# Splitting w_out beside the first convolution and loading it back in two parts

## The chip, the core and the metric

The kernel runs on one core of one Trainium2 chip. The metric is device time in microseconds (us): the median of three runs. Besides these runs there is one profiled execution, from which every line of a profile in this document comes.

## What is computed

One layer of an encoder block with two groups of heads, for a prompt of 256 tokens and a sample of 2048, each with 16 meta tokens ahead of it. Width is 1024. Cut to what matters here:

```python
h = rmsnorm(z, norm_w)
q, k, v, g_att, c_val, c_glu, g_conv = split(h @ w_in)
att = windowed_gqa(rmsnorm(q), rmsnorm(k), v, sink) * silu(g_att)      # 8 heads, 2 kv heads, window 128
u   = c_val * sigmoid(c_glu)
cnv = silu(layernorm(depthwise_conv31(u))) * silu(g_conv)
out = z + concatenate([att, cnv], -1) @ w_out                          # w_out: 1024 x 1024
```

All inputs and results are float32. The kernel computes a float32 product in three passes of TensorE: each operand is split into a rounded part (hi) and the rest (lo), and hi·hi, hi·lo and lo·hi are summed (`PASSES`, L125). A split costs one cast on ScalarE (hi) and one subtraction on VectorE (lo).

## The kernel before, in words

**Stages.** There are 18 blocks of 128 tokens, in six groups of three blocks. The first half of the work takes groups 0 to 2, the second half groups 3 to 5. In each half the columns of the input projection are taken in 11 units of 256 columns: four GLU pairs (`U_C`), two units of convolution gates (`U_GC`), two of attention gates (`U_GA`), one of k and v, two of q (`ORDER`). A unit is done for each group of its half (in the first half the first two units alternate by group). A projection is 24 matmuls into one PSUM buffer (L767, or L783 where tokens are the rows); these buffers rotate over two tags of two buffers. A GLU unit's result is multiplied on VectorE (L822), a gate's goes through SiLU on ScalarE (L875, tile `go`, three buffers) and to DRAM. The 31 taps of the convolution are VectorE instructions over 1167 tokens (L841, L850); they run beside the projections, about as many for each projection as its time allows (`tick`, with a credit in ns).

**Weights.** The split of w_in's units is made in the first half and, from the third unit on, kept in DRAM scratch (`wd`, stored in L746, loaded back in the second half in L724, four loads of 512 KB a unit).

**The last unit and the attention.** The last unit of the second half is q's second one. When it starts, the pools of the right side are closed, the attention's tiles are allocated there (`attention_open`), and the attention's first steps are laid between the unit's nine blocks (`spread`). The attention is a pipeline of slots, eight for each block: in step s, block s has its scores (L316, then `bias_max` on VectorE in L371, `expo` on ScalarE in L383, `norm` on GpSimd in L397 and L406), block s-1 has its transposes (L429), their split (L440, L441) and the product with v (L464), and block s-2 has its output projection (L538). `EARLY` is 13: so many slots are laid between the q blocks. The rest follow in `attention_rest`, where the left pools are closed and the tiles for gates, convolution results, x and y are allocated (`bp`). It first loads the first block's attention gate (`load_ga(0)`, L299) and convolution gate and result (`load_mix(0)`, L303 and L305). `mix_conv` (L515) multiplies those two on GpSimd and splits the product (L520, L521).

**w_out.** The output projection needs w_out as hi and lo in SBUF, 16 pieces of 128 x 1024. They lie in six of the tiles that held groups 3 to 5's input (`xh`, `xl` of the pool `xp`; three pieces in a tile), so they can arrive only when a group's last projection is done. `load_wo(n)` is called for row block `OUT_ORDER[n]` behind block 11 (n = 0 to 2), 14 (3 to 5) and 17 (6 and 7), by `WO_AT`. It loads two halves of 256 KB into a tile with two buffers (`woraw`, L290), and two ticks later each is cast (L294) and subtracted (L295) into place.

**Order.** Nearly all DMAs are issued by SyncE (SP), in one order, and all but a few go through one queue over the 16 DMA engines. Tile's planner decides the order of each engine by a simulated timeline with program order as the priority; an instruction in `keep_in_program_order` stays in program order on its engine. From `attention_open` on, GpSimd keeps program order (`MAN1`), and from `attention_rest` on TensorE does too (`MAN2`). An engine that waits holds up everything behind it in its order.

The tags that the change uses are `xt` (four buffers; raw transposed input for a group, loaded in `Prep.load`) and `xn` (two buffers; rows of z in `stats`, used for the sums of squares). Groups 0 to 2 are prepared at the start, groups 3 to 5 at the end of the first half, and `stats` runs in the first units and again in the attention gate units.

Of the kernel before, what the change touches and what calls it, by code (L numbers as in the profile page):

```python
# [10 lines left out]
F32 = mybir.dt.float32  # L11
F32R = mybir.dt.float32r
BF16 = mybir.dt.bfloat16
AF = mybir.ActivationFunctionType
ALU = mybir.AluOpType
AX = mybir.AxisListType

P = 128
D = 1024
# [13 lines left out]
UW = 256  # L33
# [4 lines left out]
XTB = 4  # L38
# [17 lines left out]
PIN_W = 2  # L56
I2 = 2
QP = 2
WO_AT = (3, 3, 3, 4, 4, 4, 5, 5)

GROUPS = [(0, 400)] + [(400 + 384 * i, 384) for i in range(5)]
CHUNKS = [[0, 1, 2], [3, 4, 5]]
# [13 lines left out]
def hymba_kernel(  # L76
# [24 lines left out]
    vmd = dram.tile([NM, 2 * P], F32, name="vmd")  # L101
    wd = dram.tile([11, 4, P, 4 * UW], F32, name="wd")
    cd = dram.tile([NB, P, 512], F32, name="cd")

    ident = const.tile([P, P], F32, name="ident")
    make_identity(nc, ident)
# [29 lines left out]
    def later(k, f):  # L136
        due.setdefault(clock[0] + k, []).append(f)
# [139 lines left out]
    def load_wo(n):  # L277

        e = OUT_ORDER[n]
        for hl in range(2):  # L280
            idx = 2 * n + hl
            if idx % 3 == 0:
                slot = idx // 3
                wo_slot[slot] = xp.tile([P, ND, 400], F32R, tag=("xh", "xl")[slot % 2], name=f"wo{slot}")
            flat = wo_slot[idx // 3].rearrange("p a n -> p (a n)")
            wo[e, hl] = flat[:, D * (idx % 3) : D * (idx % 3) + D]
        for nh in range(2):
            cols = slice(512 * nh, 512 * nh + 512)
            raw = pool["a"].tile([P, 512], F32, tag="woraw", name=f"woraw{n}_{nh}", bufs=2)
            nc.sync.dma_start(raw, w_out[e][:, cols])  # L290
            later(2, lambda hi=wo[e, 0][:, cols], lo=wo[e, 1][:, cols], raw=raw: split_wo(hi, lo, raw))

    def split_wo(hi, lo, raw):
        nc.scalar.copy(hi, raw)  # L294
        nc.vector.tensor_tensor(lo, raw, hi, op=ALU.subtract)  # L295

    def load_ga(b):
        gat[b] = pool["b"].tile([P, 4, P], F32, tag="ga", name=f"ga{b}", bufs=1)
# [2 lines left out]
    def load_mix(b):  # L301
        gct[b] = pool["b"].tile([P, 4, P], F32, tag="gc", name=f"gc{b}")
        nc.sync.dma_start(gct[b], gd[4:8, :, P * b : P * b + P].rearrange("j p n -> p j n"))  # L303
        cnt[b] = pool["b"].tile([P, 4, P], F32, tag="cn", name=f"cn{b}")
        nc.sync.dma_start(cnt[b].rearrange("p j n -> p (j n)"), cd[b])  # L305
# [280 lines left out]
    def spread(b):  # L586

        spread_n[0] += 1
        if spread_n[0] == QP:
            q_prep(0)  # L590
        upto = EARLY * max(0, spread_n[0] - QP) // (9 - QP)
        while len(slots) > len_all - upto:
            slot_step(*slots.pop(0))
        if b % 3 == 2:
            for n in range(8):
                if WO_AT[n] == b // 3:
                    load_wo(n)

# [2 lines left out]
    def attention_rest():  # L601
        while ln_q:
            tick(0)
        for _ in range(2):
            tick(0)
        cst["man"].close()
        att_pools.enter_context(tc.manual_schedule(engines=MAN2))
        left_pools.close()
        pool["b"] = att_pools.enter_context(tc.tile_pool(name="bp", bufs=2, side="left", reuse_waits="tile"))
        load_ga(0)  # L610
        load_mix(0)
        while slots:
            slot_step(*slots.pop(0))
        while work_left():
            tick(3000)
        att_pools.close()

    if True:
# [20 lines left out]
        class Prep:  # L639
# [50 lines left out]
            def split(self, d2):  # L690
                n, xt = self.n, self.xt[d2]
                xh, xl = xg[self.g]
                for dd in range(2):
                    d = 2 * d2 + dd
                    if self.pool:
                        nc.scalar.mul(xh[:, d, :n], xt[:, dd, :n], nw[:, d : d + 1])
                    else:
                        nc.scalar.copy(xh[:, d, :n], xt[:, dd, :n])  # L698
                for dd in range(2):
                    d = 2 * d2 + dd  # L700
                    if self.pool:
                        nc.vector.scalar_tensor_tensor(
                            xl[:, d, :n], xt[:, dd, :n], nw[:, d : d + 1], xh[:, d, :n], op0=ALU.mult, op1=ALU.subtract
                        )
                    else:
                        eng = nc.gpsimd if dd else nc.vector
                        eng.tensor_tensor(xl[:, d, :n], xt[:, dd, :n], xh[:, d, :n], op=ALU.subtract)  # L707
                owe(1000)
# [303 lines left out]
        def at_item_start(i, c, u, g):  # L1012
            if i == 0:
                r[4]()
                r[5]()
                for q in range(4):
                    preps[1].load(q)
                    w01[1][1](q, nc.gpsimd if q % 2 else nc.vector)
                r[6]()
            if i == 1:  # L1020
                later(1, preps[1].first)
                later(1, preps[1].alloc)
                later(1, lambda: preps[1].scale(0))
                for q in range(4):
                    if q < 3:
                        later(1, lambda q=q: preps[1].scale(q + 1))
                    later(1, lambda q=q: preps[1].split(q))
                for k in range(7, 10):
                    later(1, lambda k=k: later(1, stats(k)))
                for q in range(4):  # L1030
                    later(2, lambda q=q: preps[2].load(q))
            if i == I2:
                later(1, preps[2].first)
                later(1, preps[2].alloc)
                later(1, lambda: preps[2].scale(0))
                for q in range(4):
                    if q < 3:
                        later(1, lambda q=q: preps[2].scale(q + 1))
                    later(1, lambda q=q: preps[2].split(q))
# [8 lines left out]
        for i, (c, u, g) in enumerate(items):  # L1048
            if (c, u) == keys[-1] and g == CHUNKS[c][0]:
                while conv_q[0] or conv_q[1]:  # L1050
                    tick(3000)
                for _ in range(3):
                    tick(0)
                right_pools.close()
                attention_open()
            if u in U_C and g == CHUNKS[c][0]:
                u_tiles(c, u)
            ws = wsplit[c, u]
            at_item_start(i, c, u, g)
            for t, p, what in prep_at.get(i, []):  # L1060
                if what == "load":
                    for q in range(4):
                        later(1, lambda p=p, q=q: p.load(q))
                else:
                    later(1, p.first)
                    for q in range(4):
                        later(1 + q // 2, lambda p=p, q=q: p.scale(q))
            if u in U_C:
                c_group(c, u, ws, g)
            elif u in U_Q:  # L1070
                q_group(ws, u - U_Q[0], g, spread if (c, u) == keys[-1] else lambda b: None)
            elif u == U_KV:
                kv_group(ws, g)
            elif u in U_GC:
                g_group(ws, 4 + 2 * (u - U_GC[0]), g)
            else:
                g_group(ws, 2 * (u - U_GA[0]), g)
            for k in loads.get(i, []):
                load, split = weights(k)
                load(nc.sync)  # L1080
                room = max(1, when[first_at[keys[k]]] - when[i + 1])
                for q in range(4):
                    at = max(1, min(room, W0 + q * min(WST, max(1, (room - 2) // 4))))
                    later(at, lambda split=split, q=q: split(q, nc.vector))
            if c == 0 and u in U_GA:
                for k3 in range(3):
                    k = 10 + 3 * (3 * (u - U_GA[0]) + g) + k3
                    if k <= NB:
                        later(1 + k3, lambda k=k: later(1, stats(k)))
            if (c, u) == (0, ORDER[-1]):  # L1090
                p = preps[g + 3]
                p.alloc()
                for q in range(4):
                    later(1 + q // 2, lambda p=p, q=q: p.split(q))
            if u in U_C and g == CHUNKS[c][2]:
                conv(c, u, 0)
            if i == last_at[c, u] and u == U_GC[-1]:
                def ready(c=c):
                    if left[c, 0]:
                        return False  # L1100
                    seen.setdefault(c, clock[0])
                    return clock[0] >= seen[c] + LN_WAIT[c]

                for b in range(0, 8) if c == 0 else range(8, NB):
                    ln_block(c, b, ready)
# [60 lines left out]
```

## Time and profile before

| what | value |
|---|---|
| median of three runs | 976.84 us (975.87 to 977.05) |
| profiled execution, its own time | 974.79 us |
| its span, first to last instruction | 973.0 us |
| busy TensorE / VectorE / ScalarE / GpSimd | 949.2 / 755.9 / 424.6 / 341.2 us |
| mean granted TensorE clock | 0.995 |
| packets' bytes on the DMA queues | 155.75 MB |

How to read the lines: PE is TensorE's matmuls, PEld its weight loads (beside PE), DVE VectorE, ACT ScalarE, POOL GpSimd, SP SyncE; a q behind a name is the engine's sequencer, which issues DMAs. L538 is line 538 of the kernel. A line of the timeline has start, duration, engine, line, operation, output<-input by the program's names, shapes and count; in brackets stands the engine's idle time just before, and what ended it. In the view of waits the columns are total us, times and longest us. In the view by stretches each engine has its busy time and its count of instructions, then come the granted clock (1 is full speed), the mean share of the 16 DMA engines that was busy, and the rate.

### The profile page before, as it was taken

The numbers are of one execution on the slowest core, as the hardware profiler recorded it, in microseconds if no ns is written. First come the engines' busy times: TensorE is split into PE (matmuls) and PEld (weight loads), VectorE is DVE, ScalarE is ACT, GpSimd is POOL, SyncE is SP. The second block draws the span as 40 slices with busy tenths as digits, with TensorE's granted clock in tenths as the row PEclk, the third lists the DMA queues.
The fourth block names the chain that finished last, engine by engine and source line by source line (L and its number), as shares of the span: only waits on it lengthen the run. The fifth ranks groups of instructions, "written<-read, shape, count | busy, mean of one in ns | idle before, by whom it ended". The sixth has DMA issues, their size and how long they took to land.

```text
span 973.0 us, 16234 instructions
## 1 busy us (share of the span) xinstructions
PE 949.2 (98%) x5740; PEld 890.0 (91%) x5740; DVE 755.9 (78%) x1261; ACT 424.6 (44%) x1156; POOL 341.2 (35%) x541
## 2 busy tenths in 40 slices
PE   5999999999999999999999998899999999999998
PEld 5999999999999999999999998678888888888886
DVE  4759999998987699999993555877776777767772
ACT  6621111343468710111113454766665666666651
POOL 5500000364468300000002464745445544544451
PEclk9999999999999999999999998999999999999999
DMA  9643345785735222233335657954554445544321
GB/s 332 221 181 118 130 170 179 264 286 182 225 124 180 92 73 76 86 128 136 127 135 173 212 141 219 294 171 134 159 177 148 125 152 166 178 127 135 109 88 43
DMA packets 113872, 155.75 MB, mean 160 GB/s; under 512 B 10592, under 2 KB 77296, under 8 KB 113792
## 3 DMA queue, kind: packets, MB, share of 16 engines
q1 hardware_dynamic: 113648, 154.11, 48.1%
q0 software_dynamic: 144, 0.62, 0.4%
q8 instruction: 45, 0.74, 0.3%
q14 instruction: 35, 0.29, 0.1%
HBM read 101.00 MB, written 54.31 MB: 160 GB/s over the span
## 4 chain that ended last, share of the span: by engine, by line
PE 91%; DMA 3%; DVE 2%; POOL 1%; issue 1%; SPq 1%; ACT 0%; POOLq 0%; DVEq 0%
PE pj L767 42%; PE y L538 20%; PE pj L783 13%; PE O L464 5%; PE pT L429 4%; PE S L316 4%; DMA woraw<-in_w_out 2%; DMA snk<-in_sink 1%; DMA wraw<-in_w_in 1%; PE O L316 1%; PE lnt L183 1%; PE qT L316 1%; PE lnu L202 1%; PE kt L941 0%; PE pT_m L426 0%
## 5 line engine op out<-in xcount | busy, mean ns | idle before, releaser
L767 PE MATMUL pj<-xh,ws 128*128 128x384 f32 (+1 forms) x1536 | 397.2, 339 | 2.5 <-ACT xh L698 2.5
L850 DVE SCALAR_TENSOR_TENSOR y<-us,cw,y 128x1167 f32<-128x1167 f32 x240 | 329.0, 1428 | 0.6
L767 PEld LDWEIGHTS pj<-xh,ws 128*128 128x128 f32 x1536 | 282.3, 189 | 2.8 <-ACT xh L698 2.8
L767 PE MATMUL pj<-xl,ws 128*128 128x384 f32 (+1 forms) x768 | 262.5, 342 | 0.1
L783 PE MATMUL pj<-ws,xh 128*128 128x256 f32 (+1 forms) x880 | 165.8, 286 | 0.0
L767 PEld LDWEIGHTS pj<-xl,ws 128*128 128x128 f32 x768 | 144.7, 188 | 1.1 <-POOL xl L707 0.7
L783 PEld LDWEIGHTS pj<-ws,xh 128*128 128x128 f32 (+1 forms) x880 | 137.8, 189 | 0.3
L783 PE MATMUL pj<-ws,xl 128*128 128x256 f32 (+1 forms) x440 | 125.4, 285 | 0.0
L383 ACT ACTIVATE sb<-sb,nm 128x304 f32<-128x304 f32 (+4 forms) x144 | 77.1, 535 | 45.3 <-DVE nm L371 43.7
L538 PE MATMUL y<-wo,mch 128*128 128x512 f32 x288 | 95.9, 414 | 0.0
L538 PE MATMUL y<-wo,mah 128*128 128x512 f32 x288 | 93.7, 406 | 0.0
L441 DVE TENSOR_TENSOR pl<-pT,ph 128x512 fp32r<-128x512 f32 x100 | 69.0, 690 | 29.0 <-ACT ph L440 28.5
L875 ACT ACTIVATE go<-pj 128x384 f32<-128x384 f32 x48 | 23.6, 491 | 154.5 <-PE pj L767 145.3
L371 DVE CUSTOM_DVE_ANT_0 sb<-S,bias,nsnk 128x304 f32<-128x304 f32 (+4 forms) x144 | 73.5, 511 | 15.0 <-PE S L316 14.5
L783 PEld LDWEIGHTS pj<-ws,xl 128*128 128x128 f32 (+1 forms) x440 | 83.2, 189 | 0.2
L122 POOL TENSOR_SCALAR ssk<-ssk 128x2 f32<-128x2 f32 x18 | 6.4, 356 | 213.0 <-ACT sqk L889 212.9
L440 ACT CAST ph<-pT 128x512 fp32r<-128x512 f32 x100 | 58.2, 583 | 40.2 <-PE pT L429 39.5
L406 POOL TENSOR_SCALAR sb<-sb,es 128x304 f32<-128x304 f32 (+4 forms) x144 | 72.8, 525 | 3.6
L316 PEld LDWEIGHTS S<-kw,q 128*128 128x128 f32 x288 | 53.8, 191 | 17.9 <-DVE nm L371 5.9
L122 POOL TENSOR_SCALAR ssq<-ssq 128x4 f32<-128x4 f32 (+2 forms) x55 | 28.3, 515 | 114.4 <-ACT xn L632 76.9
L316 PE MATMUL S<-kw,q 128*128 128x304 f32 (+4 forms) x288 | 62.6, 299 | 5.3 <-DVE nm L371 5.3
L429 PE MATMUL pT<-ident,sb 128*128 128x128 f32 x400 | 61.6, 274 | 1.3 <-POOL sb L406 1.0
(118 smaller groups left out, 1441.8 us busy)
## 6 DMA issues: line engine op xcount, KB each, us to landing
wd<-ws SPq DMA_DIRECT2D x36, 512.0 KB, 5.7
ws<-wd SPq DMA_DIRECT2D x36, 512.0 KB, 5.3
wraw<-in_w_in SPq DMA_DIRECT2D x52, 256.0 KB, 5.6
xn<-in_z SPq DMA_DIRECT2D x18, 512.0 KB, 5.7
gd<-go SPq DMA_DIRECT2D x48, 192.0 KB, 2.1
yo<-in_z SPq DMA_DIRECT2D x36, 256.0 KB, 2.6
out_y<-yo SPq DMA_DIRECT2D x36, 256.0 KB, 2.4
kw<-kd SPq DMA_DIRECT2D x16, 512.0 KB, 5.7
```

The lines of the kernel that those rows point to most:

```text
L316: r = f(*a, **k)
L371: nc.vector.tensor_tensor_reduce(out=sb[:, n, c0:c1], in0=ps[:, 0:w], in1=cst["bias"][:, kv, n, c0 - QB * n : c1 - QB * n], scale=1.0, sca ...
L383: nc.scalar.activation(sb[:, n, c0:c1], sb[:, n, c0:c1], AF.Exp, bias=nm[:, n : n + 1], scale=-1.0, accum_out=rs[:, n : n + 1],)
L406: nc.gpsimd.tensor_scalar(sb[:, k, a0:a1], sb[:, k, a0:a1], es[:, k : k + 1], 1.0, op0=ALU.mult, op1=ALU.mult)
L429: nc.tensor.transpose(pt[:, hl, :], sbt[b, kv][:, hl, KCOL[k] : KCOL[k] + P], ident)
L440: nc.scalar.copy(ph, pt)
L441: nc.vector.tensor_tensor(pl, pt, ph, op=ALU.subtract)
L464: nc.tensor.matmul(o, lhs, t, start=(start and i == 0), stop=(stop and i == 1))
L538: nc.tensor.matmul(ps, mh[mi][:, e % 4, :], wo[e, wi][:, cols], start=(e == 4 and k == 0), stop=(e == 3 and k == 2),)
L767: nc.tensor.matmul(ps[:, :n], ws[:, d, wi, P * half_i : P * half_i + P], x[xi][:, d, o : o + n], start=(k == 0), stop=(k == 3 * ND - 1),)
L783: nc.tensor.matmul(ps[:rows, :UW], x[xi][:, d, o : o + rows], ws[:, d, wi, :], start=(k == 0), stop=(k == 3 * ND - 1),)
L850: nc.vector.scalar_tensor_tensor(y[:, yo + o0 : yo + o1], u[:, o0 + k : o1 + k], cw[:, j, k : k + 1], y[:, yo + o0 : yo + o1], op0=ALU.mul ...
```

## The change

`load_wo` no longer splits anything. A new function, `split_wo(e)`, does it during the first half, at the start of the items of groups 0 and 1 in units 3 to 6 (`U_C[2]`, `U_C[3]`, both `U_GC`): eight items, one for each row block of w_out. It loads the two raw halves into `xt` buffers, in program order on SP; two ticks later it casts hi into an `xn` buffer and subtracts lo in place, and one tick after that stores both to a new DRAM scratch tensor `wod`. `load_wo` loads hi and lo from there straight into their place, 512 KB each. Six row blocks are loaded behind blocks 11 and 14, as before; the last two (four loads) are loaded in `attention_rest`, behind `load_ga(0)` and `load_mix(0)`, and no longer behind block 17.

```diff
-WO_AT = (3, 3, 3, 4, 4, 4, 5, 5)
+WO_AT = (3, 3, 3, 4, 4, 4)
...
+    wod = dram.tile([8, 2, P, D], F32, name="wod")
...
             wo[e, hl] = flat[:, D * (idx % 3) : D * (idx % 3) + D]
+            nc.sync.dma_start(wo[e, hl].bitcast(F32), wod[e, hl])
+
+    def split_wo(e):
+
+        raw = [sp.tile([P, 2, 400], F32, tag="xt", name=f"woraw{e}_{nh}", bufs=XTB)[:, :, :UW] for nh in range(2)]
         for nh in range(2):
-            cols = slice(512 * nh, 512 * nh + 512)
-            raw = pool["a"].tile([P, 512], F32, tag="woraw", name=f"woraw{n}_{nh}", bufs=2)
-            nc.sync.dma_start(raw, w_out[e][:, cols])
-            later(2, lambda hi=wo[e, 0][:, cols], lo=wo[e, 1][:, cols], raw=raw: split_wo(hi, lo, raw))
-
-    def split_wo(hi, lo, raw):
-        nc.scalar.copy(hi, raw)
-        nc.vector.tensor_tensor(lo, raw, hi, op=ALU.subtract)
+            src = w_out[e][:, 512 * nh : 512 * nh + 512].rearrange("p (a n) -> p a n", n=UW)
+            tc.keep_in_program_order(nc.sync.dma_start(raw[nh], src))
+
+        def split():
+            hi = sp.tile([P, D], F32R, tag="xn", name=f"wohi{e}")
+            for nh in range(2):
+                part = hi[:, 512 * nh : 512 * nh + 512].rearrange("p (a n) -> p a n", n=UW)
+                nc.scalar.copy(part, raw[nh])
+                nc.vector.tensor_tensor(raw[nh].bitcast(F32R), raw[nh], part, op=ALU.subtract)
+                dst = wod[e, 1][:, 512 * nh : 512 * nh + 512].rearrange("p (a n) -> p a n", n=UW)
+                later(1, lambda nh=nh, dst=dst: nc.sync.dma_start(dst, raw[nh]))
+            later(1, lambda: nc.sync.dma_start(wod[e, 0], hi.bitcast(F32)))
+
+        later(2, split)
...
         if b % 3 == 2:
-            for n in range(8):
+            for n in range(len(WO_AT)):
                 if WO_AT[n] == b // 3:
                     load_wo(n)
...
         load_ga(0)
         load_mix(0)
+        for n in range(len(WO_AT), 8):
+            load_wo(n)
         while slots:
...
             at_item_start(i, c, u, g)
+            if c == 0 and u in (U_C[2], U_C[3], U_GC[0], U_GC[1]) and g != 2:
+                split_wo(2 * (U_C + U_GC).index(u) - 4 + g)
```

## The prediction

> **What bounds the kernel now.** I read the page's head first, then the stretches around the first use of w_out, then who waited there.
>
> ```profile
> span 973.0 us, 16234 instructions
> PE 949.2 (98%) x5740; PEld 890.0 (91%) x5740; DVE 755.9 (78%) x1261; ACT 424.6 (44%) x1156; POOL 341.2 (35%) x541
> PE 91%; DMA 3%; DVE 2%; POOL 1%; issue 1%; SPq 1%; ACT 0%; POOLq 0%; DVEq 0%
> ```
>
> TensorE is busy 98% of the span and is 91% of the chain that ended last. No matmul is removed or added, so only the missing 2% and the slow clock can move. The view by stretches (width, then busy time of PE, PEld, DVE, ACT, POOL, then granted clock, DMA share, GB/s) shows where they are:
>
> ```profile
> 592.00:600.00 8.00, 4.58 (x38) 4.38 (x36) 1.70 (x6) 2.10 (x5) 0.20 (x1) 0.91 0.94 293
> 600.00:608.00 8.00, 8.00 (x49) 8.00 (x49) 6.54 (x21) 5.25 (x16) 6.63 (x11) 0.67 0.62 198
> 608.00:616.00 8.00, 6.65 (x53) 6.12 (x52) 5.85 (x19) 5.84 (x17) 4.15 (x8) 1.00 0.82 235
> 616.00:624.00 8.00, 5.40 (x26) 3.41 (x26) 7.88 (x23) 7.16 (x23) 6.71 (x9) 1.00 0.94 291
> 624.00:632.00 8.00, 7.10 (x30) 5.51 (x30) 7.44 (x15) 5.01 (x11) 6.18 (x10) 0.79 1.10 358
> 648.00:656.00 8.00, 6.41 (x36) 5.21 (x35) 4.46 (x14) 3.31 (x10) 4.15 (x7) 1.00 0.50 166
> ```
>
> PE's holes are 3.42, 1.35, 2.60, 0.90 and 1.59 us, 9.9 us in all. The clock costs another 8 x 0.33 = 2.64 us in the second stretch and 8 x 0.21 = 1.68 us in the fifth. This is all that an edit of the transition can win: about 14 us. Who waits, between 592 and 655 us (total, times, longest), and the longest case in the timeline:
>
> ```profile
> ACT wo L294 <- DMA woraw<-in_w_out: 12.6, 11, 6.2
> DVE wo L295 <- ACT wo L294: 9.0, 5, 6.3
> PE S L316 <- DVE nm L371: 5.3, 3, 3.4
> PE pT_m L426 <- POOL pm L397: 1.6, 1, 1.6
> ```
> ```profile
> 597.66 0.62 ACT L294 CAST wo<-woraw 128x512 fp32r<-128x512 f32 x1 [6.16 <-DMA woraw<-in_w_out]
> 598.30 0.69 DVE L295 TENSOR_TENSOR wo<-woraw,wo 128x512 fp32r<-128x512 f32 x1 [6.30 <-ACT wo L294]
> 599.44 0.52 PE L316 MATMUL S<-kw,q 128*128 128x176 f32 x1 [3.42 <-DVE nm L371]
> ```
>
> The cast of w_out stands in ScalarE's order ahead of its data, VectorE's subtraction stands behind the cast, and the score matmul waits for a PSUM buffer that VectorE would free next. That is the first hole, and the slow clock follows it.
>
> **The change part by part.** *Removed from the transition:*
>
> ```profile
> L290 SPq DMA_DIRECT2D woraw<-in_w_out x16: 327/333/1389, 593.1 to 637.2; - x16
> L294 ACT CAST wo<-woraw x16: 617/618/622, 597.7 to 639.8; 128x512 fp32r<-128x512 f32 x16
> L295 DVE TENSOR_TENSOR wo<-woraw,wo x16: 683/693/1766, 598.3 to 640.5; 128x512 fp32r<-128x512 f32 x16
> ...
> DMA to landing us min/median/max: 2.5/3.8/6.2
> ```
>
> 16 casts x 0.618 = 9.9 us of ScalarE, 16 subtractions x 0.693 = 11.1 us of VectorE, with their waits, and 16 loads of 256 KB (4.2 MB). If nothing else became late, the holes and the slow clock up to 624 us would go: 3.42 + 1.35 + 2.60 + 2.64 = 10.0 us. I count on at most 8, since the 2.60 us hole also holds the chain of scores, maximum, exponential and scaling that stays.
>
> *Added to the transition:* 16 loads of 512 KB (8.4 MB): twelve from load_wo in the last projection unit, four after load_ga(0) and load_mix(0). They need no engine but the queue. So what is late next is a transfer. The first output projection waits for this:
>
> ```profile
> 620.41 1.46 POOL L515 TENSOR_TENSOR cn<-cn,gc 128x512 f32<-128x512 f32 x1 [0.21 <-DMA cn<-cd]
> 621.84 0.84 POOL L397 TENSOR_TENSOR pm<-sb,es 128x128 f32<-128x128 f32 x1
> 622.78 1.74 POOL L406 TENSOR_SCALAR sb<-sb,es 128x272 f32<-128x272 f32 x4
> ```
> ```profile
> 623.34 1.57 PE L429 MATMUL pT<-ident,sb 128*128 128x128 f32 x4 [1.04 <-POOL sb L406]
> 624.66 0.71 PE L538 MATMUL y<-wo,mch 128*128 128x512 f32 x2
> 626.13 0.79 PE L538 MATMUL y<-wo,mcl 128*128 128x512 f32 x1 [0.75 <-DVE mcl L521]
> ```
>
> GpSimd's order is the program's here: mix_conv(0) (L515) stands ahead of the scaling (L406) that the next transposes (L429) need, and the first projection stands behind these on PE. So y cannot begin before cn(0) has landed plus about 4.3 us (624.66 - 620.41), however early the rest is. Its load on SP:
>
> ```profile
> 611.15 0.47 SPq L299 DMA_DIRECT2D ga<-gd  x1
> 611.67 0.60 SPq L303 DMA_DIRECT2D gc<-gd  x1
> 615.21 0.34 SPq L290 DMA_DIRECT2D woraw<-in_w_out  x1
> 615.60 0.43 SPq L159 DMA_DIRECT2D qd<-qs  x1
> 616.08 0.43 SPq L305 DMA_DIRECT2D cn<-cd  x1
> ```
>
> Now SP stands between gc and cn until a woraw buffer is free; that goes. But by program order, and by when their buffers come free, all twelve 512 KB loads are issued ahead of ga, gc and cn. Their price is from a burst of four loads of that size and row length, ws<-wd, and the transfers already there from the two stretches of the transition:
>
> ```profile
> 362.50:375.00 12.50, 12.50 (x73) 12.50 (x73) 12.07 (x11) 0.49 (x1) 0.00 (x0) 1.00 0.46 168
> 593.00:611.00 18.00, 14.58 (x102) 14.38 (x102) 10.49 (x31) 10.21 (x28) 7.21 (x11) 0.81 0.77 237
> 611.00:634.00 23.00, 18.14 (x94) 13.73 (x92) 20.85 (x53) 16.52 (x45) 17.15 (x26) 0.93 0.98 305
> ```
>
> 168 / 0.46 = 365 GB/s at full share; 12 x 0.524 MB = 6.29 MB take 17.2 us. From 593 to 611 the queue did 0.77 x 18 = 13.9 us of work for 4.27 MB; eight woraw loads (2.1 MB) are about half, 6.8 us, and 7.1 us remain. ga, gc and cn: 0.79 MB at 305 / 0.98 = 311 GB/s, 2.5 us. Together 26.8 us from 593.06, where w_out's loads begin: 619.9, and with 1 us for the signal (an estimate: the quickest woraw load took 2.5 us to land, of which 0.8 is its own work) 620.9. At the share of 1.10 that the queue reached from 624 to 632 it is 593.06 + 24.4 + 1 = 618.5. L515 would then start between 618.5 and 620.9 instead of 620.41; I take the middle, 0.7 us earlier. So most of the 8 us won before this point is waited away on cn(0).
>
> By the Trainium skill (HBM Reference, Specifications (TRN2)) a core that streams alone reaches about 425 GB/s; the burst above shows 365. At 425 the twelve loads would take 14.8 us, an estimate, and the total would be 2.4 us lower.
>
> After that point: the wait for mcl (0.75 us) goes, as VectorE has nothing else to do while cn is awaited. The hole at 648 us (1.59 us, PE on POOL on VectorE's es) goes too, since five subtractions, 3.5 us, leave VectorE after 632 us. On the other side PE stands idle for several us before the first y; the stretch 600 to 608 shows what follows a 3.4 us hole, 2.64 us, against 1.68 us now: +0.96. Sum: -0.7 - 0.75 - 1.59 + 0.96 = -2.1 us.
>
> *Added beside the first convolution:* per row block two loads of 256 KB, two casts, two subtractions and three stores (two of 256 KB, one of 512); eight blocks, in the third to sixth unit of the first half. The first row below is a piece of the chain that ended last, 24 of whose matmuls make a projection: 24 x 181.98 / 1031 = 4.24 us. The second is the last gate of the sixth unit. Four units of six projections before it begin at about 69 us.
>
> ```profile
> 39.28 181.98 PE pj L767 x1031
> ```
> ```profile
> 170.68 0.49 ACT L875 ACTIVATE go<-pj 128x384 f32<-128x384 f32 x1 [3.73 <-PE pj L767]
> ```
>
> I price casts and subtractions like those removed. The stretch and the one behind it:
>
> ```profile
> 69.00:170.00 101.00, 101.00 (x573) 101.00 (x572) 99.78 (x93) 18.22 (x34) 4.05 (x3) 1.00 0.45 159
> 170.00:337.00 167.00, 167.00 (x1207) 166.17 (x1206) 139.35 (x190) 89.82 (x321) 90.40 (x118) 1.00 0.57 192
> ```
>
> ScalarE has room (18 of 101). VectorE has 1.2 us for 11.1, so it falls behind by up to 9.9 us; it makes that up after 170 us, where 27.7 us are free. PE does not notice while the lag stays under three projections, since it rotates four PSUM buffers: 3 x 4.24 = 12.7 us. I cost it at nothing; without that cover it is at most the 9.9 us. The queue gets 4.2 MB of loads and 8.4 MB of stores, 34 us at 365 GB/s beside 45 us of 101: it fits. On SP, 24 stores can stand waiting for VectorE and 16 loads keep program order, each waiting for its xt buffer and, at a unit's start, behind four weight loads. Behind them stand the gate stores (three buffers, again three projections of cover) and weight loads that have a unit of 25 us (6 x 4.24). Between 0 and what exceeds the cover; I take 0.
>
> The profiled execution took 974.79 us (span 973.0 and 1.8 around it), 2.05 below the median of the three runs. The sum gives 972.7 for it; on the median, 976.84 - 2.1 = 974.8.
>
> **The rivals.** *The transfers keep up.* If gc and cn get ahead of some of the w_out loads, or these run faster, y starts when the engines are ready: 8 us gained in all, 968.8. For it: queue share is only 0.62 from 600 to 608. Against it: that gap is itself SP waiting for woraw buffers. By the 425 GB/s of the Trainium skill alone it would be 972.4.
>
> *The gate loads land late.* From 608 to 616 the queue moved 235 GB/s at 0.82, 287 at full share. At that rate the twelve loads take 21.9 us, 4.7 more, and every us of cn's landing after 619.4 (26.3 us of queue work from 593.06) is a us of y: 976.84 - 2.1 + 4.7 = 979.4. For it: small rows (kw, qd, gates) mix with the loads. Against it: 358 GB/s from 624 to 632 with the same mix.
>
> *VectorE becomes the bound at the convolution.* If half of the 9.9 us shows as PE waits, because a subtraction waits in order for a late cast: 974.8 + 5 = 979.8. For it: VectorE is busy 98.8% there. Against it: PE waits nowhere in that stretch and the cover is 12.7 us.
>
> By the Trainium skill (TensorE: Matmul & The Clock Gate, What's actually happening) the clock halves after an idle window of about 3.4 us and returns after a busy one; the dip after the 3.42 us hole agrees. By it the restart costs, as an estimate, 1.7 to 3.4 us instead of 2.64, which moves the sum by -0.9 or +0.8.
>
> **How the numbers follow.** Forecast 0.46, at 974.8, own range 972.5 to 977.5. Transfers keep up 0.20 (968.8); gate loads late 0.20 (979.4); VectorE 0.14 (979.8). 0.2% is 1.95 us, about what a measurement of this kernel can tell from no change: faster means under 974.9. The forecast splits 0.23 faster, 0.21 same, 0.02 slower; the first rival is all faster; the second 0.16 slower, 0.04 same; the third 0.12 slower, 0.02 same. Faster 0.43, same 0.27, slower 0.30. The range 968.5 to 981.0 leaves out 0.08 below and 0.12 above.
>
> **What would show it.** Right: no PE hole at 596, DMA share about 1 from 593 to 620, POOL L515 waiting for cn<-cd several us, and y starting within 2 us of 624.66. Wrong: L515 not waiting and y at 616 (first rival); L515 after 623 (second); PE waiting on DVE between 69 and 250 us (third).

## The result

| kernel | median, us | runs | against the kernel before |
|---|---|---|---|
| before | 976.84 (975.87 to 977.62) | 5 | |
| changed | 981.39 (979.59 to 987.0) | 5 | 1.0053, 95% interval 1.003 to 1.0075 |

The change makes the kernel slower by about 5.2 us (2.9 to 7.3; the ratio times 977 us, while the two medians are 4.6 apart). The prediction was 974.8 us, and the range's upper end, 981.0, lies just below the median. The profiled executions took 979.59 us (changed) and 974.79 us (before). Both are among the faster ones of their kernel, so sizes are taken from medians below, and the traces say where the time goes. One run of the kernel before in a later series took 2412.38 us, a slow one that the ratios leave out.

**The profile after.** The page's head, with the first line of the chain that ended last:

```profile
span 977.7 us, 16281 instructions
PE 949.5 (97%) x5740; PEld 889.6 (91%) x5740; DVE 754.4 (77%) x1261; ACT 427.1 (44%) x1158; POOL 346.3 (35%) x541
PE 90%; DMA 5%; DVE 3%; issue 1%; POOL 1%; SPq 0%; ACT 0%; DVEq 0%; POOLq 0%; ACTq 0%
```

TensorE has the same work (949.5 us against 949.2), so the 4.7 us of span are holes and slow clock. In the chain DMA has grown from 3% to 5%. The transition, by stretches (width, then busy time of PE, PEld, DVE, ACT, POOL, granted clock, DMA share, GB/s):

```profile
592.00:600.00 8.00, 8.00 (x71) 8.00 (x70) 3.05 (x12) 5.43 (x15) 3.46 (x6) 1.00 0.73 223
600.00:608.00 8.00, 8.00 (x69) 7.80 (x68) 4.25 (x15) 3.67 (x12) 4.51 (x9) 1.00 0.99 358
608.00:616.00 8.00, 5.53 (x37) 4.39 (x36) 5.32 (x19) 4.13 (x15) 3.31 (x7) 1.00 1.04 411
616.00:624.00 8.00, 5.43 (x24) 4.14 (x23) 6.24 (x18) 5.68 (x15) 5.31 (x9) 0.79 1.07 376
624.00:632.00 8.00, 2.07 (x4) 1.26 (x5) 3.06 (x7) 1.43 (x3) 2.64 (x3) 0.52 1.07 376
632.00:640.00 8.00, 8.00 (x39) 6.80 (x39) 3.11 (x9) 3.37 (x10) 5.83 (x8) 0.84 1.10 352
```

The hole from 596 to 599.4 us is gone, with the slow clock behind it. In its place the queue is full from 600 us on, and PE is busy only 2.07 of the 8 us from 624 to 632, at a clock of 0.52. What PE and GpSimd waited for there, in the timeline:

```profile
619.79 1.73 POOL L418 TENSOR_SCALAR sb<-sb,es 128x272 f32<-128x272 f32 x4
627.91 1.26 POOL L527 TENSOR_TENSOR cn<-cn,gc 128x512 f32<-128x512 f32 x1 [6.38 <-DMA cn<-cd]
...
633.35 1.27 POOL L527 TENSOR_TENSOR cn<-cn,gc 128x512 f32<-128x512 f32 x1 [2.81 <-DMA cn<-cd]
```
```profile
621.49 0.60 PE L441 MATMUL pT<-ident,sb 128*128 128x128 f32 x4
629.87 1.22 PE L550 MATMUL y<-wo,mch 128*128 128x512 f32 x2 [7.79 <-ACT mch L532]
```

L527 is the product that was L515, L418 the scaling that was L406, L441 the transposes that were L429, and L550 the output projection; mch is the hi part of the product, cast in L532. GpSimd waits 6.38 us for block 0's cn, PE 7.79 us for what is made of it. The scaling and the transposes, which stood behind this product before, are now done ahead of it, so y begins 2.0 us after GpSimd takes up cn (before, 4.3).

A smaller hole comes from other transfers. Buffers of scaled q (qs) come free when their stores to DRAM (qd) have landed, and these stores stand among the w_out loads. VectorE's wait for them from 590 to 640 us (total, times, longest), and the score matmul behind its longest case, which needs the PSUM buffer that VectorE frees when it makes the maxima (nm) after that:

```profile
DVE qs L917 <- DMA qd<-qs: 9.0, 3, 4.2
```
```profile
611.04 0.47 PE L328 MATMUL S<-kw,q 128*128 128x208 f32 x2 [2.08 <-DVE nm L383]
```

SP's issues of w_out and of the gates:

```profile
597.02 4.32 SPq L288 DMA_DIRECT2D wo<-wod  x6
...
607.87 3.43 SPq L288 DMA_DIRECT2D wo<-wod  x6
...
617.91 0.32 SPq L288 DMA_DIRECT2D wo<-wod  x1
619.16 0.37 SPq L311 DMA_DIRECT2D ga<-gd  x1
619.89 0.81 SPq L315 DMA_DIRECT2D gc<-gd  x1
621.69 0.33 SPq L317 DMA_DIRECT2D cn<-cd  x1
623.11 1.28 SPq L288 DMA_DIRECT2D wo<-wod  x3
```

Thirteen of the sixteen loads stand ahead of cn, which is issued 5.6 us later than before (3.6 of them were lost ahead of the transition, as shown below) and lands at 627.8.

**The first half** has a loss of its own. VectorE's groups between 69 and 170 us (count, busy us, mean ns, idle before), first of the kernel before, then of the changed one:

```profile
L850 DVE SCALAR_TENSOR_TENSOR y<-us,cw,y 128x1167 f32<-128x1167 f32 x63 | 86.0, 1424 | 0.0
```
```profile
L864 DVE SCALAR_TENSOR_TENSOR y<-us,cw,y 128x1167 f32<-128x1167 f32 x56 | 77.2, 1424 | 0.0
L302 DVE TENSOR_TENSOR woraw<-woraw,wohi 128x512 fp32r<-128x512 f32 x16 | 10.5, 681 | 0.7 <-ACT wohi L301 0.7
```

The sixteen subtractions push seven of 63 taps out of the stretch. When are they made up? The same taps over the whole first half, with the first and the last start, before and after:

```profile
L850 DVE SCALAR_TENSOR_TENSOR y<-us,cw,y x120: 1412/1427/1437, 62.9 to 282.8; 128x1167 f32<-128x1167 f32 x120
```
```profile
L864 DVE SCALAR_TENSOR_TENSOR y<-us,cw,y x120: 1412/1425/1434, 63.8 to 295.1; 128x1167 f32<-128x1167 f32 x120
```

Not before the last tap: it starts 12.3 us later, and the first only 0.9. By then the q units run, which need VectorE for each block. The stretches from 170 to 300 us before, the last of them after, and what TensorE waited for between 170 and 340 us in the changed kernel (total us, times, longest; before, it waits for nothing there):

```profile
170.00:250.00 80.00, 80.00 (x537) 79.30 (x536) 71.07 (x77) 31.57 (x96) 37.58 (x40) 1.00 0.67 233
250.00:300.00 50.00, 50.00 (x427) 49.99 (x426) 40.18 (x64) 29.40 (x147) 32.66 (x46) 1.00 0.59 187
```
```profile
250.00:300.00 50.00, 47.89 (x403) 47.26 (x402) 46.66 (x65) 26.57 (x133) 33.14 (x41) 1.00 0.58 183
```
```profile
PE pj L797 <- DVE qs L917: 1.1, 1, 1.1
PE lnt L184 <- DVE xt L695: 0.8, 1, 0.8
PE pj L797 <- DVE kn L944: 0.2, 1, 0.2
```

From 250 us on VectorE goes from 40.2 to 46.7 busy us, and PE loses 2.1. With the activations of gates and GLUs matched one by one, the changed kernel's trace is 3.6 us behind from 360 us to the transition, of which 0.8 us arose before 50 us and the rest, 2.8 us, between 240 and 360. The last projection ends 4.6 us later, so in this pair of executions the transition adds 1.0.

### The profile page after: what moved, and what is told of

Read it like the earlier page. It is cut to its first block, busy times and chain, and to the rows that moved or that the text cites. A ratio compares the mean times of both kernels' runs of the same rounds, so it can differ in the third digit from the quotient of the medians.

```text
span 977.7 us, 16281 instructions
## 1 busy us (share of the span) xinstructions
PE 949.5 (97%) x5740; PEld 889.6 (91%) x5740; DVE 754.4 (77%) x1261; ACT 427.1 (44%) x1158; POOL 346.3 (35%) x541
## 4 chain that ended last, share of the span: by engine, by line
PE 90%; DMA 5%; DVE 3%; issue 1%; POOL 1%; SPq 0%; ACT 0%; DVEq 0%; POOLq 0%; ACTq 0%
PE pj L781 42%; PE y L550 20%; PE pj L797 12%; PE O L476 5%; PE pT L441 4%; PE S L328 4%; DMA qd<-qs 1%; DMA kw<-kd 1%; DMA snk<-in_sink 1%; PE O L328 1%; DMA wraw<-in_w_in 1%; PE lnt L184 1%; DVE y L864 1%; PE lnu L203 1%; PE qT L328 1%
## 5 line engine op out<-in xcount | busy, mean ns | idle before, releaser
L797 PE MATMUL pj<-ws,xh 128*128 128x256 f32 (+1 forms) x880 | 163.6, 284 | 1.3 <-DVE qs L917 1.1
L797 PEld LDWEIGHTS pj<-ws,xh 128*128 128x128 f32 (+1 forms) x880 | 135.8, 187 | 2.2 <-DVE qs L917 1.3
L550 PE MATMUL y<-wo,mch 128*128 128x512 f32 x288 | 96.6, 417 | 7.8 <-ACT mch L532 7.8
L550 PE MATMUL y<-wo,mah 128*128 128x512 f32 x288 | 93.7, 406 | 0.0
L418 POOL TENSOR_SCALAR sb<-sb,es 128x304 f32<-128x304 f32 (+4 forms) x144 | 70.5, 508 | 3.6
L123 POOL TENSOR_SCALAR ssq<-ssq 128x4 f32<-128x4 f32 (+2 forms) x55 | 30.5, 555 | 112.8 <-ACT xn L646 77.2
L517 POOL TENSOR_TENSOR at<-at,ga 128x256 f32<-128x256 f32 x36 | 27.1, 753 | 102.1 <-DVE at L511 102.1
```

The costliest lines, as they stand in the source:

```text
L418: nc.gpsimd.tensor_scalar(sb[:, k, a0:a1], sb[:, k, a0:a1], es[:, k : k + 1], 1.0, op0=ALU.mult, op1=ALU.mult)
L550: nc.tensor.matmul(ps, mh[mi][:, e % 4, :], wo[e, wi][:, cols], start=(e == 4 and k == 0), stop=(e == 3 and k == 2),)
L797: nc.tensor.matmul(ps[:rows, :UW], x[xi][:, d, o : o + rows], ws[:, d, wi, :], start=(k == 0), stop=(k == 3 * ND - 1),)
```

## The experiments

The theory was that the loss is in two places, VectorE's lag in the first half and cn behind the w_out loads in the transition. Each run stands beside runs of the kernel before on the same chip, and a difference in us is the ratio's times 977 us.

**One part alone.** The first kernel keeps the early split and its stores, but loads and splits w_out in the transition as before:

```diff
-WO_AT = (3, 3, 3, 4, 4, 4)
+WO_AT = (3, 3, 3, 4, 4, 4, 5, 5)
...
-            nc.sync.dma_start(wo[e, hl].bitcast(F32), wod[e, hl])
+        for nh in range(2):
+            cols = slice(512 * nh, 512 * nh + 512)
+            raw = pool["a"].tile([P, 512], F32, tag="woraw", name=f"woraw{n}_{nh}", bufs=2)
+            nc.sync.dma_start(raw, w_out[e][:, cols])
+            later(2, lambda hi=wo[e, 0][:, cols], lo=wo[e, 1][:, cols], raw=raw: split_late(hi, lo, raw))
```

> The first half of the change alone: w_out is split beside the first convolution and stored as in the changed kernel, but nothing reads these parts; the transition loads and splits w_out as the kernel before did. Theory (two places: about 2.8 us where VectorE's 11 us of added subtractions reach TensorE at 250 to 292 us, 0.8 us at the start, and a net 1.0 us in the transition): about 980.4 us, 3.6 over the kernel before, with TensorE waiting on VectorE at 250 to 292 us. Rival A (the transition alone makes the loss, the shift of the first half is chance): 976.8, as before. Rival B (the first half makes all of it): 981.4, as the changed kernel.

Measured: 981.49 us against 977.22, ratio 1.0049 (1.0035 to 1.0062): 4.8 us, all of the change's loss, as rival B says; the theory's 980.4 lies at the lower end of the interval. Its trace has the same waits, a little longer:

```profile
PE lnt L184 <- DVE xt L703: 1.6, 1, 1.6
PE pj L805 <- DVE qs L925: 1.5, 1, 1.5
```

Matched by the same activations, this trace falls back 5.3 us between 240 and 360 us, where the changed kernel's fell back 2.8 and that of a kernel below with the same first half (block 0's gc and cn ahead) 3.8. So single traces of this loss differ by some 2 us, around the 4.8 of the medians.

The second kernel has only the loads:

```diff
-            nc.sync.dma_start(wo[e, hl].bitcast(F32), wod[e, hl])
+            nc.sync.dma_start(wo[e, hl].bitcast(F32), wd[CACHE + e, hl])
...
-            if c == 0 and u in (U_C[2], U_C[3], U_GC[0], U_GC[1]) and g != 2:
-                split_wo(2 * (U_C + U_GC).index(u) - 4 + g)
```

> The second half of the change alone: nothing of w_out is split, and the sixteen loads of 512 KB of the changed kernel stand where they stand there, but fetch parts of w_in of the same size and row length from the scratch that exists already; so the output projection multiplies by the wrong weights. Theory (two places): about 977.8 us, the transition's net loss of 1.0 without the first half's 3.6, with GpSimd's product of cn waiting for its load as long as in the changed kernel (9 us in all). Rival A (the transition alone): 981.4. Rival B (the first half alone): 976.8 or less, down to 968.8 if the transition wins what its waits cost before.

Measured: 976.68 against 977.22, ratio 1.0000 (0.999 to 1.001), rival B again, with the theory's loss of 1.0 at the edge of the interval. The new transition neither wins nor loses, and not because nothing happens in it: PE's first projection there waits 8.3 us for mch.

```profile
PE S L328 <- DVE nm L383: 3.4, 1, 3.4
```
```profile
628.42 1.22 PE L550 MATMUL y<-wo,mch 128*128 128x512 f32 x2 [8.35 <-ACT mch L532]
```
```profile
626.46 1.26 POOL L527 TENSOR_TENSOR cn<-cn,gc 128x512 f32<-128x512 f32 x1 [6.76 <-DMA cn<-cd]
```

So the two halves add up: 4.8 and 0.0 against 5.2. The theory's second place is not seen as a loss; what the old holes cost is waited away.

**Which part of the early split costs?** Two kernels. The first moves the subtractions to GpSimd:

```diff
-                nc.vector.tensor_tensor(raw[nh].bitcast(F32R), raw[nh], part, op=ALU.subtract)
+                nc.gpsimd.tensor_tensor(raw[nh].bitcast(F32R), raw[nh], part, op=ALU.subtract)
```

> The changed kernel, with the sixteen subtractions of the early split on GpSimd, which is busy 4 of 101 us there, in place of VectorE. Theory: the lag of VectorE goes, TensorE no longer waits at 250 to 292 us, and the time falls by about 2.8 us to 978.6. Rival E (not the subtractions but the loads and stores of the split, or the tiles that they borrow, delay the first half): within 0.5 us of the changed kernel, 981.4.

Measured: 983.63 us, ratio 1.0067 (1.0055 to 1.008). Neither expectation held; it is no faster than the change, since VectorE gets slower beside GpSimd. VectorE's and GpSimd's rows of this kernel, VectorE's from 69 to 170 us, and the same subtraction on GpSimd at the start of the kernel before:

```profile
L864 DVE SCALAR_TENSOR_TENSOR y<-us,cw,y 128x1167 f32<-128x1167 f32 x54 | 85.3, 1633 | 0.0
```
```profile
L302 POOL TENSOR_TENSOR woraw<-woraw,wohi 128x512 fp32r<-128x512 f32 x16 | 47.3, 2977 | 40.7 <-ACT wohi L301 28.6 <-DMA woraw<-in_w_out 12.1
```
```profile
L743 POOL TENSOR_TENSOR ws<-wraw,ws 128x512 fp32r<-128x512 f32 x4 | 5.6, 1408 | 3.9 <-ACT ws L742 3.9
```

A tap takes 1633 ns on the mean instead of 1424, so only 54 fit: 54 x 0.209 = 11.3 us more, which is more than the 10.5 us of subtractions taken away. So VectorE is no less late, and the run can't tell what its lag costs. The next kernel takes the subtractions away and leaves every transfer:

```diff
-                nc.vector.tensor_tensor(raw[nh].bitcast(F32R), raw[nh], part, op=ALU.subtract)
...
-                later(1, lambda nh=nh, dst=dst: nc.sync.dma_start(dst, raw[nh]))
+                later(1, lambda part=part, dst=dst: nc.sync.dma_start(dst, part.bitcast(F32)))
```

> The changed kernel without the sixteen early subtractions: the low part is left out and a copy of the high part stands in its place, so the loads, casts and stores of the early split, and their bytes, stay as they are. Theory now (VectorE starts the q units some 14 us late with its convolution, because it never has the slack to catch up, and TensorE waits for it there): the first half's loss of about 4.5 us goes, 977 us. Rival (the 12.6 MB of early loads and stores delay other transfers): 981, as the changed kernel.

Measured: 978.46 against 976.82, ratio 1.0015 (1.0007 to 1.0024). About 3.7 of the 5.2 us go with the subtractions (3.3 beside the kernel with the early split alone), and the waits at 250 to 292 us with them:

```profile
PE pj L796 <- DVE qs L916: 0.3, 1, 0.3
```

The kernel with the loads alone has the same 0.3 us wait. The remaining 1.5 us (0.7 to 2.4) have no place in the first half of this trace: between 60 and 360 us it falls back 0.5 us, as much as that of the kernel with the loads alone, which splits nothing. It is 1.1 us behind before 50 us already, but so are five traces (0.6 to 1.6 us) of the seven kernels below whose code for the first half is that of the kernel before. So the casts, loads and stores of the early split are not shown to cost anything there, and where the 1.5 us arise stays open.

**The same split elsewhere.** First where VectorE has most room, from 493 to 560 us:

```diff
-            if c == 0 and u in (U_C[2], U_C[3], U_GC[0], U_GC[1]) and g != 2:
-                split_wo(2 * (U_C + U_GC).index(u) - 4 + g)
+            late = [(1, U_GA[1], 4), (1, U_GA[1], 5)] + [(1, u2, g2) for u2 in (U_KV, U_Q[0]) for g2 in CHUNKS[1]]
+            if (c, u, g) in late:
+                split_wo(late.index((c, u, g)))
```

> The changed kernel with the same split moved into the second half, one row block per group from the last gate unit through the key and value unit to the first q unit (about 493 to 560 us), where VectorE is busy 10 to 12 of every 20 us from 500 us on. Theory (the cost is VectorE's lag where it is full): about 977 us, as the kernel that only loads. Rival (the split costs about 4.5 us wherever it stands): 981.

Measured: 987.54, ratio 1.0121 (1.0105 to 1.0137), the slowest of all, far above both expectations. VectorE has room there, the queue has not. Its stretches (the DMA share, last but one, is 0.52 and 0.70 there in the kernel before) and waits from 590 to 650 us:

```profile
520.00:540.00 20.00, 20.00 (x173) 20.00 (x172) 14.75 (x27) 8.68 (x39) 7.11 (x15) 1.00 0.98 318
540.00:560.00 20.00, 18.86 (x162) 18.64 (x161) 12.01 (x27) 10.81 (x34) 8.02 (x16) 1.00 0.97 325
```
```profile
POOL cn L527 <- DMA cn<-cd: 12.0, 2, 8.3
...
POOL sb L245 <- DMA wod<-woraw: 7.9, 1, 7.9
```

The attention's tiles take the place of the split's, and GpSimd, which clears them, waits 7.9 us for the split's last stores. At 520 us this trace is only 0.4 us behind that of the kernel before, at its end 10.2 (983.2 against 973.0); how the loss is shared between the full queue and this wait isn't separated.

Then into the same four units of the second half, where the queue is 0.3 busy and VectorE nearly as full as in the first half, but with free time coming before the q units:

```diff
-            if c == 0 and u in (U_C[2], U_C[3], U_GC[0], U_GC[1]) and g != 2:
-                split_wo(2 * (U_C + U_GC).index(u) - 4 + g)
+            if c == 1 and u in (U_C[2], U_C[3], U_GC[0], U_GC[1]) and g != 5:
+                split_wo(2 * (U_C + U_GC).index(u) - 7 + g)
```

> The changed kernel with the same split, two row blocks per unit in the same four units, but of the second half (about 360 to 430 us), where the queue is 0.3 busy and no q unit follows until VectorE has had its free time of 10 us in 20 from 510 us on. Theory (the split costs only where VectorE's lag of some 14 us, or a full queue, runs into a unit that waits for it): 977 us, as the kernel that only loads. Rival (the lag reaches the key and value unit and the normalisation there as well): 980 to 982.

Measured: 978.99 against 977.45, ratio 1.0019 (1.001 to 1.0028). The same sixteen subtractions and transfers cost 1.9 us instead of about 5. VectorE makes its lag up where it had free time: from 500 to 540 us it is busy 31.5 us (before, 20.9), and TensorE waits for it nowhere from 340 to 590 us in this trace, which is 1.4 us behind at 360 us and still 1.4 at 520. The result lies between the theory's 977 and the rival's 980 to 982; the 1.9 us are not in the stretch of the split, and their place stays open.

**What holds the first projection?** Half the bytes first, on the kernel that only loads:

```diff
+            if hl:
+                wo[e, 1] = wo[e, 0]
+                continue
             nc.sync.dma_start(wo[e, hl].bitcast(F32), wd[CACHE + e, hl])
```

> As the kernel that only loads (no split at all, parts of w_in in place of w_out), but with the eight loads of the high parts alone, 4.2 MB instead of 8.4; the low parts are left out and the high ones are used in their place, with the same matmuls. Theory (the transition gains nothing since the queue's bytes ahead of the first blocks' cn hold the projections): the 8 us wait for cn goes and the time falls to 968 to 971 us. Rival (the scores' chain or the clock's restart holds the projections as long anyway): 975 to 977.

Measured: 968.42, ratio 0.9925 (0.9913 to 0.9938), 7.3 us faster, with the same engine work as the kernel with all loads. GpSimd has block 0's cn at 616.33 us instead of 626.46, and y starts at 619.96 instead of 628.42:

```profile
616.33 1.27 POOL L530 TENSOR_TENSOR cn<-cn,gc 128x512 f32<-128x512 f32 x1 [1.40 <-DMA cn<-cd]
```
```profile
619.96 1.20 PE L553 MATMUL y<-wo,mch 128*128 128x512 f32 x2
```

So the queue holds it, and what the transition could win is shown too. Is it the sum of the bytes, or the order? First only block 0's gc and cn go ahead, on the changed kernel:

```diff
+        load_mix(0)
         cst["vm"] = vm = ap.tile([P, KV, P], F32R, tag="vm", name="vm", bufs=1)
...
+        p, one = (pool["a"], dict(bufs=1)) if b == 0 else (pool["b"], {})
-        gct[b] = pool["b"].tile([P, 4, P], F32, tag="gc", name=f"gc{b}")
+        gct[b] = p.tile([P, 4, P], F32, tag="gc", name=f"gc{b}", **one)
...
-        load_mix(0)
```

> The changed kernel, with block 0's gc and cn in the pool that the attention opens first, so that they are loaded ahead of the w_out loads. Theory (cn, queued behind twelve to thirteen 512 KB loads, holds the first output projection): y begins about 8 us earlier, GpSimd's product waits for nothing, and the time falls by the 7.8 us wait and part of the slow clock behind it, to about 972 us. Rival C (the q stores behind the same loads hold VectorE and the scores, so y gains little): 979 to 981. Rival D (the first weights of w_out themselves come late then): TensorE waits for wo in place of mch, 976 to 980.

Measured: 980.49, ratio 1.0039 (1.0027 to 1.0052), hardly better than the changed kernel. The time is in rival C's range, but not for its reason: y starts at 624.8 us, 5.1 earlier. The next cn is then the late one, and PE waits almost as long behind it (7.14 us against 7.79), for what GpSimd does after that cn:

```profile
634.73 1.26 POOL L529 TENSOR_TENSOR cn<-cn,gc 128x512 f32<-128x512 f32 x1 [4.08 <-DMA cn<-cd]
```
```profile
624.80 0.70 PE L552 MATMUL y<-wo,mch 128*128 128x512 f32 x2
...
636.40 0.48 PE L440 MATMUL pT_m<-ident,pm 128*128 128x128 f32 x1 [7.14 <-POOL pm L411]
```

Next, with the split in the second half, the last four w_out loads go behind block 1's gates as well:

```diff
         if slot == (3 if s_ > 1 else 6) and has_a and s_ > 0:
             load_mix(a)
+            if a == 1:
+                for n in range(6, 8):
+                    load_wo(n)
...
-        for n in range(len(WO_AT), 8):
-            load_wo(n)
```

> The split in the second half as in the run before, and two transfers reordered in the transition: block 0's gc and cn are loaded with the first loads of the attention, and the last four w_out loads stand behind block 1's gc and cn. Theory (not the total of the bytes but which small loads stand behind the 512 KB loads decides): TensorE's wait of about 8 us goes for blocks 0 and 1, 970 to 973 us. Rival (the queue has the same bytes to move before the first projections can end, whatever the order): 976 to 978.

Measured: 974.93 against 977.45, ratio 0.9976 (0.9966 to 0.9986), between the theory and the rival. The third kernel moves two more row blocks behind the first gates:

```diff
-WO_AT = (3, 3, 3, 4, 4, 4)
+WO_AT = (3, 3, 3, 4)
...
         load_ga(0)
+        for n in range(len(WO_AT), 6):
+            load_wo(n)
```

> As the run before, with two more row blocks moved behind block 0's gate load, so that eight instead of twelve 512 KB loads are issued before it. Theory (small loads ahead): another 1 to 2 us, 969 to 972. Rival (those two blocks are then late themselves for their turn in the first projection): 973 to 977, with TensorE waiting for wo.

Measured: 973.57 against 977.45, ratio 0.9966 (0.9954 to 0.9978), faster than the kernel before and the changed one. It is 1.0 us less than the run before by the ratios, though their intervals overlap; the time lies at the lower end of the rival's range, but its sign, TensorE waiting for w_out, is missing. The order is worth 5.2 us beside the same kernel without it (0.9966 against 1.0019). TensorE waits for no w_out load and for no mch; the largest waits left are small:

```profile
PE pT_m L440 <- POOL pm L411: 2.9, 2, 1.7
PE qT L330 <- DMA q<-qd: 2.2, 1, 2.2
```

It stays 4.0 us short of half the bytes (3.3 won against 7.3). Of these, 1.9 are what the split costs here and the half-bytes kernel doesn't have; the other 2.1 may be the bytes, which no run separates.

A mixture reaches for fewer bytes: three row blocks split early, five on the spot as before.

```diff
+PRE = 3
...
+            if n < PRE:
+                nc.sync.dma_start(wo[e, hl].bitcast(F32), wod[e, hl])
+        for nh in range(0 if n < PRE else 2):
...
+            late = [(1, U_KV, g2) for g2 in CHUNKS[1]]
+            if (c, u, g) in late:
+                split_wo(OUT_ORDER[late.index((c, u, g))])
```

> A mixture: three of the eight row blocks are split early, in the key and value unit of the second half, and loaded in parts; the other five are loaded whole and split in the transition as in the kernel before. 5.8 MB instead of 4.2 or 8.4 in the transition, and ten casts and subtractions instead of sixteen or none. Theory (the early casts cost stalls, the bytes cost the wait for cn; three blocks take away the first stall for 1.6 MB more): 972 to 975 us. Rival (any block that is still split on the spot stalls the engines as before): 977 to 979.

Measured: 979.87, ratio 1.0027 (1.0017 to 1.0037), above both ranges and next to the rival's. The projection now waits for casts of w_out, and the three splits fill the queue where the late split did (share 0.92 and 0.93 from 520 to 560 us):

```profile
PE y L561 <- ACT wo L298: 2.5, 1, 2.5
```

Since both are in this kernel, it doesn't tell how much each costs.

Last, VectorE's waits for the stores of q, which stand in SP's order among the big loads (9.0 us in the changed kernel):

```diff
-                    qs = gp.tile([P, 4, HD], F32, tag="qs", name=f"qs{qi}_{b}")
+                    qs = gp.tile([P, 4, HD], F32, tag="qs", name=f"qs{qi}_{b}", bufs=4)
```

> The fastest version so far (split in the second half, small loads ahead of the w_out loads), with four instead of three buffers for the scaled q that wait for their stores. There VectorE stood 9.3 us in four waits for these stores in the transition, as it stood 9.0 us in three in the changed kernel. Theory (the queue's bytes decide, and these waits lie beside the wait for cn): 973 to 974 us, no change. Rival C (VectorE, held by the stores of q, delays the maxima of the scores and with them TensorE): 970.5 to 972.5.

Measured: 974.58 against 976.61, ratio 0.9977 (0.9966 to 0.9987), no gain over the 0.9966 without it. One more buffer does not take the wait away:

```profile
DVE qs L921 <- DMA qd<-qs: 7.2, 1, 7.2
```

In this trace, of the slowest of its eight runs, TensorE stands 4.1 us behind that wait, for a buffer that the maxima free, as it stood 2.1 us in the changed kernel and 3.4 in the one with the loads alone. So the run doesn't speak against rival C's mechanism; the stores of q do hold TensorE, and what that costs the kernel isn't priced.

## Why the prediction was wrong

**The step that failed: "VectorE has 1.2 us for 11.1, so it falls behind by up to 9.9 us; it makes that up after 170 us, where 27.7 us are free ... I cost it at nothing."** The lag was right (10.5 us of subtractions, seven taps). That it is made up at no cost was wrong: the last tap starts 12.3 us later. Little of the 27.7 us free between 170 and 337 us could be used without TensorE waiting. 8.9 of them lie before 250 us (80 - 71.07), mostly as waits for weight casts that stand in VectorE's order; the changed kernel has 72.89 busy us there, only 1.8 more. The other 18.8 lie in the q units, where the late taps land: from 250 to 300 us VectorE does use 6.5 us more, and TensorE waits for it. The waits of VectorE from 170 to 250 us before:

```profile
DVE ws L743 <- ACT ws L742: 6.4, 3, 2.7
```

The cover of three projections was counted for the gate units; in the q units VectorE has to serve each block before its buffer comes free. Without the subtractions 3.7 of the 5.2 us go; where the other 1.5 us arise is open. The third rival had the right kind of price (5 us), but its place, 69 to 250 us, was too early: TensorE waits on VectorE only from 258 us on.

**The transition was right in what comes late, and two terms of its sum were wrong.** The hole at 596 us and its slow clock went, the queue is full from 600 us, and GpSimd waits 6.38 us for cn, as the forecast said. The forecast was -2.1 us, the kernel with the loads alone shows 0.0 (-1.0 to +1.0). The term that was too small is cn's landing. From the first w_out load to it I summed 27.8 us (593.06 to 620.9), or 25.4 at the higher share, and took the middle, 26.6; the trace has 30.8 us (597.02 to 627.8). One load more than twelve stands ahead of cn. The term that was too large is the step from there to y, 4.3 us, since I took GpSimd's scaling and the transposes to stand behind cn. They are done at 619.79 and 621.49 us, ahead of it, and y begins 2.0 us after GpSimd takes cn up (627.91 to 629.87). About 4.1 us too little and 2.3 too much leave 1.8, near the 2.1 us that were missed; that y was not later still is luck. The forecast also counted the hole between 608 and 616 us as gone with the casts. There TensorE now waits 2.08 us, since VectorE waits for stores of q: small transfers behind the large loads again.

A landing so late meets the second rival's condition, over 26.3 us of queue work. Its price above the forecast, 4.7 us, was too high against the 2.1 measured, since not every us of cn's landing became a us of y.

**The first rival fell as a forecast, and its price was good:** the run with half the bytes took 968.42 us, 7.3 us less by its ratio, where the rival said 968.8 and 8. What the old holes cost can be had for the most part, but only if the queue has room for what replaces them.

**The rate of the queue** was taken from a burst at 365 GB/s. The full stretches here have 352 to 411, so it was no bad choice. By the Trainium skill (HBM Reference, Specifications (TRN2)) a core that streams alone reaches about 425 GB/s; the 411 from 608 to 616 us comes near it, and yet cn came late. The rate was not what failed.

## What to carry to other kernels

Free time of an engine, summed over a long stretch, is no place for work that is late: look for where the lag ends, by the last instruction of the delayed kind, and whether a unit in which others wait for that engine lies ahead of that point. Loading split data doubles the bytes of a load; where the queue is already at 0.8 to 1.0, that replaces a wait for an engine with a wait for the queue, and small loads that something waits for belong ahead of the large ones. Moving the same split to units with a quiet queue and free time behind them, and the gates ahead of the loads, turned 5.2 us lost into 3.3 us won.

## What the runs showed of the hardware

**GpSimd and VectorE slow each other.** In the run with the subtractions on GpSimd, the middle one of the sixteen takes 2424 ns, where the same shape took 1408 on the mean at the start of the kernel before (the mean of 2977 is raised by one of 11861). VectorE's taps, which read two tiles of SBUF, take 1633 ns on the mean instead of 1424. Where they meet first, three taps take 7.24 us instead of 4.3:

```profile
75.97 9.02 POOL L302 TENSOR_TENSOR woraw<-woraw,wohi 128x512 fp32r<-128x512 f32 x4 [3.78 <-DMA woraw<-in_w_out]
```
```profile
76.61 7.24 DVE L864 SCALAR_TENSOR_TENSOR y<-us,cw,y 128x1167 f32<-128x1167 f32 x3
```

By the Trainium skill (SBUF — State Buffer, Who interferes with whom) a VectorE instruction with two SBUF inputs contends with a GpSimd instruction that reads SBUF; these rows agree. It isn't always VectorE that gives way: the subtraction of 11861 ns starts at 148.67 us, and the seven taps that VectorE starts beside it from then to 157 us take 1.42 us each, by the profile.

**Single executions differ by 2 to 3 us.** The kernel before took 975.45 to 978.67 us in 22 runs of one series, and traces of kernels with the same code up to 60 us are between 0.2 us ahead and 1.6 us behind it by then. An effect of 1 or 2 us read from one trace against another is no finding.
